# Hyena spectra laid out with two phases side by side, each piece moved by one transfer of 128 partitions, and more projection products ahead of the first spectrum

## The chip, the cores and the metric

The kernel runs on one core of one Trainium2 chip. Its time is the device time of one execution in microseconds (us); it is the median of several executions. A profile is one further execution, recorded by the hardware profiler. The core has a matrix engine (TensorE, PE in the profile; PEld is its weight load), three elementwise engines (VectorE, DVE; ScalarE, ACT; GpSimd, POOL), a queue engine (SyncE, SP), and 16 DMA engines that move data between main memory (HBM) and the on-chip memory. A DMA is issued from a queue (here SP's, or ACT's) and is carried out by DMA engines. On-chip tiles have up to 128 partitions (rows).

## What is computed

One layer of a hybrid encoder for 2048 positions of width 1024, all in float32. The part that the change touches is the Hyena group: 512 channels, a convolution over the whole length by FFT, gated, twice in a row (order 2), with filters that a small sine network makes.

```python
u = rms_norm(h); proj = u @ w_in                         # 1024 -> 3600 columns
hy = short_conv(proj[:, :1536])                          # v, gate 1, gate 2
spec = rfft(two-sided filter, length 4096)               # sine FFN times a decay window, 2 orders
z = hy[:, :512]
for o, gate in enumerate((hy[:, 512:1024], hy[:, 1024:1536])):
    conv = irfft(rfft(z, n=4096) * spec[o], n=4096)[:2048]
    z = gate * (conv + z * skip[o])
y_hy = group_rms_norm(z)
# beside it: an mLSTM group of 4 heads; then output projection, cross-attention, MLP, final norm
```

## The kernel before

Every large product is split into three TensorE products (`mm3`, L357, L360, L361: high by high, low by high, high by low part), 128 x 128 weights against 512 columns. The order in which the program is written is made by `weave` (end of the listing): two generators run in turn, each yields an amount of work, and the one that is behind by its own total goes on. The filters (`filters`) are woven into the first projection sweeps with the weights 140 and 102, and `hyena` into the rest of the projection and the mLSTM's preparation with 499 and 297. A `yield 24` in `hyena` (L1000) therefore lets the other generator go ahead by 24/297 x 499 = 40 of its units before the first spectrum; 1 unit was meant as about 1 us. A scheduler then orders the instructions of each engine.

**The FFT.** Length 4096 is split into 64 frequencies k (of 32 rows n) and 64 residues. Position = 64 n + 16 q + j: q is the phase (0 to 3), j the residue (0 to 15). The steps are:

1. `filters`, function `front`: for a pair of residues j2 (two values of j) and an order o, four banks of TensorE (one for each phase) give 128 rows: 64 rows of frequencies for each of the two residues. They are copied into two tiles `st[h]`, each with phases 2h and 2h + 1 side by side (128 partitions x 2 x 512), and `by_phase` (L339) stores them into the scratch tensor `fs`. Eight pairs, two orders, two tiles: 32 tiles of 512 KB.
2. `hyena`, function `spectrum` (L988): the same for the signal, from tiles that `load1` (L924) reads from `hy`, into the scratch `zs`. 16 tiles for each order; h = 0 is stored from ACT's queue, h = 1 from SP's.
3. The loop over 16 blocks of frequencies: `load_filter` and `load2` (L931, L939) read a block of `fs` and of `zs` (function `of_block`, L908), two products with a table (`c_dm`) finish the transform over the 64 residues, the filter is multiplied in, a product with `c_em` goes back, and `back` (L978) stores the block to the scratch `zg` from ACT's queue. A block needs all residues of its frequencies, so the first block waits for every store of step 2.
4. The loop over eight pairs of residues: `load3` (L963) reads two tiles of `zg` through `by_phase`, and a gate tile from `hy`; the product with `e2` finishes the inverse; the gate is multiplied in. For order 0 the result goes straight into `spectrum(1, ...)`, for order 1 it is normalised and stored to `yh` (L1064).

**The scratch layout before** is (64 frequencies, 4 phases, 16 residues, 512 channels). A tile of `by_phase` has the two residues in its two partition halves, so it is moved by two transfers of 64 partitions, with two rows of 2 KB to each partition. `of_block` is moved by two transfers of 64 partitions too, one for each frequency parity g; the tiles of `hy` and `yh` by four transfers of 32 partitions, one for each phase.

The tile pools matter: `filters` has 7 tiles of 512 KB (`ta`), of which the decay windows hold up to 4, and `hyena` has 10. A tile that is being stored cannot be used again before the store has landed.

A place that the change leaves alone, but that the prediction uses: `halves` in the preparation of the memory tokens (L679 to L685) loads eight pieces of 64 KB from the scratch `rows` into quarters of the tile `rp`. In the tile a piece has 32 partitions; in the scratch it is read as 4 groups with a step of their own, of 8 rows of 2 KB each: `by_half = rows.rearrange("i (d s n h) t -> s (i d) n (h t)", d=2, s=2, n=8)`, then `dma_start(out=rp[32 * q:32 * q + 32, s], in_=by_half[s])`.

Of the kernel before, what the change touches and what calls it, by code (L numbers as in the profile page):

```python
# [21 lines left out]
CH = 512  # L22
# [6 lines left out]
def shape_constants():  # L29
    f32 = np.float32  # L30
    ang = f32(TWO_PI / L) * np.arange(L, dtype=f32)
    tl = np.linspace(0.0, 1.0, L, dtype=f32)
    bands = np.linspace(1e-4, 15, 16, dtype=f32)
    arg = bands[:, None] * ang[None, :]
    feat = np.concatenate([tl[None], np.cos(arg), -np.sin(arg)], axis=0).astype(f32)
    back = (L - np.arange(L)) % L
    c_feat = np.concatenate([feat, feat[:, back]], axis=0)

    lo = math.log(1e-2) / 1.5
    hi = math.log(1e-2) / 0.3  # L40
    deltas = np.abs(np.linspace(lo, hi, CH, dtype=f32))
    win = np.exp(-(tl[:, None] * deltas[None, :]).astype(np.float64)).astype(f32)
    winb = win[back].copy()
    winb[0] = 0.0
    c_win = np.stack([win, winb], 0).reshape(2, 32, 4, 16, CH).transpose(0, 2, 1, 3, 4).reshape(2, L, CH)

    n1 = np.arange(32)
    kk = np.arange(16)
    f1 = np.zeros((2, 32, 4, 16, 2, 4))
    for par in range(2):  # L50
        th = 2 * np.pi * ((n1[:, None] * (2 * kk + par)[None, :]) % 64) / 64
        for h in range(4):
            f1[par, :, h, :, 0, h] = np.cos(th)
            f1[par, :, h, :, 1, h] = -np.sin(th)
            if par == 0:
                f1[0, :, h, 0, 1, h] = 1.0 - 2.0 * (n1 % 2)
    f1 = f1.reshape(2, 128, 128)
    wgt = np.full((2, 16, 2, 4), 2.0)
    wgt[0, 0] = 1.0
    e2 = f1.transpose(0, 2, 1) * (wgt.reshape(2, 128, 1) / 4096.0)  # L60
    own = f1.reshape(2, 32, 4, 16, 2, 4)[:, :, 0, :, :, 0].transpose(1, 0, 2, 3).reshape(32, 64)
    inv = e2.reshape(2, 16, 2, 4, 32, 4)[:, :, :, 0, :, 0].reshape(64, 32)

    n2 = np.arange(64)
    k2 = np.arange(64)

    def block(freq):
        th = 2 * np.pi * ((n2[:, None] * freq[None, :]) % 4096) / 4096
        return np.cos(th), np.sin(th)

    dm = np.zeros((32, 2, 64, 2, 64))
    for par in range(2):
        for k in range(16):
            k1 = 2 * k + par
            b = dm[par * 16 + k]
            if k1 > 0:
                c, s = block(k1 + 64 * k2)
                b[0, :, 0], b[1, :, 0], b[0, :, 1], b[1, :, 1] = c, s, -s, c
            else:
                c, s = block(64 * k2[:32])  # L80
                b[0, :, 0, :32], b[0, :, 1, :32] = c, -s
                b[0, :, 1, 0] = 1.0 - 2.0 * (n2 % 2)
                c, s = block(32 + 64 * k2[:32])
                b[1, :, 0, 32:], b[1, :, 1, 32:] = c, -s
    dm = dm.reshape(32, 128, 128)
    em = dm.transpose(0, 2, 1).copy()
    two = np.full((128, 1), 2.0)
    two[0] = two[64] = 1.0
    em[0] *= two
    c = {  # L90
        "c_feat": c_feat,
        "c_win": c_win,
        "c_f1": np.tile(own, (4, 1)),
        "c_e2": np.tile(inv, (2, 1)),
        "c_dm": dm.transpose(1, 0, 2),
        "c_em": em.transpose(1, 0, 2),
    }
    return {k: np.ascontiguousarray(v.astype(np.float32)) for k, v in c.items()}
# [30 lines left out]
class Prog:  # L129
# [101 lines left out]

    def filters(self):
        nc, tc, a = self.nc, self.tc, self.a
        sd = [self.dram(f"fs{o}", (64, 4, 16, CH)) for o in range(2)]
        sb, ta, tb = self.fsb, self.ta, self.tb
        if True:
            fw = sb.tile([128, 1280], F32, name="fw")
# [79 lines left out]
            for j2 in range(8):  # L317
                yield 9
                (wf, wb), nxt = nxt, windows(j2 + 1)
                for o in range(2):  # L320
                    st, es = [ta() for h in range(2)], []
                    for jj in range(2):
                        j = 2 * j2 + jj
                        pf, pb = self.hy(), self.hy()
                        self.beside((pf, hid[0:64, j], w3[0:64, o]), (pb, hid[64:128, j], w3[64:128, o]))
                        f, b = tb(), tb()
# [10 lines left out]
        self.fes.close()  # L337

    def by_phase(self, queue, d, j2, h, t, load=False):  # L339
        for jj in range(2):  # L340
            at, own = d[:, 2 * h:2 * h + 2, 2 * j2 + jj], t[64 * jj:64 * jj + 64]
            queue.dma_start(out=own if load else at, in_=at if load else own)

    def filters_open(self):
        self.fes = ExitStack()
# [554 lines left out]
    def hyena(self, es):  # L900
        nc, tc, a = self.nc, self.tc, self.a
        hy = self.dram("hy", (3, L, CH)).rearrange("s (n q j) c -> s q n j c", q=4, j=16)
        yh = self.dram("yh", (L, CH)).rearrange("(n q j) c -> q n j c", q=4, j=16)
        fs, sds, gds = ([self.dram(f"{n}{o}", (64, 4, 16, CH)) for o in range(2)] for n in ("fs", "zs", "zg"))
        own = [slice(64 * g, 64 * g + 64) for g in range(2)]
        phase = [slice(32 * q, 32 * q + 32) for q in range(4)]

        def of_block(d, g, k):  # L908
            return d[2 * k + g:2 * k + g + 3:2].rearrange("k q j c -> (q j) k c")

        sb = es.enter_context(tc.tile_pool(name="h_sb", bufs=1))

# [11 lines left out]
        def load1(j2):  # L924
            z = ta()
            js = slice(2 * j2, 2 * j2 + 2)
            for q in range(4):
                nc.sync.dma_start(out=z[phase[q]], in_=hy[0, q, :, js])
            return z

        def load_filter(o, i):  # L931
            dm = sb.tile([128, 2, 128], F32, tag="dm", name="dm", bufs=3)
            nc.sync.dma_start(out=dm, in_=a["c_dm"][:, 2 * i:2 * i + 2])
            t = ta()
            for g in range(2):
                nc.sync.dma_start(out=t[own[g]], in_=of_block(fs[o], g, 2 * i))
            return dm, t

        def load2(o, i):  # L939
            em = sb.tile([128, 2, 128], F32, tag="em", name="em", bufs=2)  # L940
            nc.sync.dma_start(out=em, in_=a["c_em"][:, 2 * i:2 * i + 2])
            t = ta()
            for g in range(2):
                nc.sync.dma_start(out=t[own[g]], in_=of_block(sds[o], g, 2 * i))
            return em, t

        def response(i, dm, t):
# [14 lines left out]
        def load3(o, j2):  # L962
            js = slice(2 * j2, 2 * j2 + 2)  # L963
            r = [ta() for h in range(2)]
            for h in range(2):
                self.by_phase(nc.sync, gds[o], j2, h, r[h], True)
            gate = ta()
            for q in range(4):
                nc.sync.dma_start(out=gate[phase[q]], in_=hy[1 + o, q, :, js])
            return r, gate  # L970

        held = []
# [7 lines left out]
        def back(m, i, em, y, gs, dst):  # L980
            pg = self.hy()
            nc.tensor.matmul(pg, em[:, m], y, start=True, stop=True)  # L982
            nc.scalar.copy(gs[:, m], pg)
            if m == 1:
                for g in range(2):
                    nc.scalar.dma_start(out=of_block(dst, g, 2 * i), in_=gs[own[g]])

        def spectrum(o, j2, z):  # L988
            st = [ta() for h in range(2)]
# [7 lines left out]
                self.by_phase(nc.sync if h else nc.scalar, sds[o], j2, h, st[h])  # L997

        q, fq = [load1(0), load1(1)], []
        yield 24  # L1000
        self.strict = True
        for j2 in range(8):
            yield 3.5
# [6 lines left out]
        for o in range(2):  # L1010
# [4 lines left out]
            for i in range(16):  # L1015
                yield 4.6
                dm, hr, hi = ready
                em, t = nxt
# [19 lines left out]
            for j2 in range(8):  # L1038
                yield 4.5 if o else 6.0
                js = slice(2 * j2, 2 * j2 + 2)  # L1040
                r, gate = nxt
                if j2 < 7:
                    nxt = load3(o, j2 + 1)
                pp = [self.hy() for jj in range(2)]
                self.beside(*((pp[jj][phase[q]], e2[own[jj]], r[q // 2][own[jj], q % 2])
                              for jj in range(2) for q in range(4)), pin=True)
                for jj in range(2):
                    nc.vector.tensor_tensor(gate[:, jj], pp[jj], gate[:, jj], ALU.mult)
                if o == 0:
                    late(lambda j2=j2, gate=gate: spectrum(1, j2, gate))  # L1050
                    if j2 > 5:
                        fq.append(load_filter(1, j2 - 6))
                    continue
                y = gate.rearrange("q j (g e) -> q (j g) e", g=8)
                sq = ta()
                sqv = sq.rearrange("q j (g e) -> q (j g) e", g=8)
                nc.gpsimd.tensor_tensor(sqv, y, y, ALU.mult)
                ms = sb.tile([128, 16], F32, tag="ms", name="ms", bufs=2)
                nc.vector.tensor_reduce(ms, sqv, AX.X, ALU.add)
                rv = self.bank_rsqrt(sb, ms, 64)  # L1060
                nc.vector.tensor_tensor(sqv, y, rv.unsqueeze(2).broadcast_to([128, 16, 64]), ALU.mult)
                for jj in range(2):
                    nc.gpsimd.tensor_tensor(sq[:, jj], sq[:, jj], ghy, ALU.mult)
                for q in range(4):  # L1064
                    nc.sync.dma_start(out=yh[q, :, js], in_=sq[phase[q]])
            late(None)

    def gates_open(self, es):
# [1026 lines left out]
def program(p):  # L2095
    with ExitStack() as ms:
        with ExitStack() as es:
# [15 lines left out]
            with ExitStack() as hs:  # L2113
# [2 lines left out]
                             among(chain(p.natural(0, (0, 1)), p.sweep((6, 7), 0, False),  # L2116
                                         p.natural(0, (2,), p.prep_mem, 2)), p.states(), 1),
                             p.turned_in(), take(n, 1), beside_each(n, take(m, 5)))
                weave(rest, p.hyena(hs), 499, 297, True)
            for _ in rest:  # L2120
                pass
        with ExitStack() as rs:
# [65 lines left out]
```

## Time and profile before

| | |
|---|---|
| median of 3 executions | 3109.29 us (3103.45 to 3109.89) |
| the profiled execution | 3107.95 us, of which its span is 3105.9 us |
| TensorE busy | 2983.7 us, 96% of the span |
| VectorE, ScalarE, GpSimd busy | 1945.9, 1496.0, 1124.2 us |
| moved by DMA | 607.08 MB, 195 GB/s over the span |
| mean granted TensorE clock | 0.983 |

The lines of the profile that are quoted below are of these kinds. A line of a table of windows has, for each engine, its busy time in that stretch and the number of instructions, then the TensorE clock that was granted, the mean busy share of the 16 DMA engines (it can pass 1 where packets overlap), and the GB/s that they moved. A line of one tile's instructions has the line of the kernel, the engine (SPq and ACTq are the DMA queues of SP and ACT, and the duration is that of the issue, not of the transfer), the number, the least, median and longest duration in ns, and the first and last start in us. A line of a DMA queue has its packets, its MB and the time that the packets took, as a share of 16 engines over the stretch asked for. A timeline's line has start, duration, engine, line, operation, and in brackets the idle time before it with what ended it.

### The profile page before, as it was taken

The page shows a single profiled execution, that of the slowest core. Times are in us where ns is not written, and L with a number is a line of the kernel's source. Part 1 is how long each engine was busy: PE and PEld are TensorE (multiplying, and loading weights), DVE is VectorE, ACT ScalarE, POOL GpSimd, SP SyncE. Part 2 cuts the span into 40 slices and gives each one's busy share as a digit, 9 for nine tenths or more (in the row PEclk, how much of TensorE's full clock was granted, in tenths as well). Part 3 has the DMA queues.
Part 4 walks back from the last instruction along what each step waited for, and adds up shares of the span by engine and source line. Part 5 has one row for each costly group of instructions (what it writes and reads, how often), then busy time and mean ns, then how long its engine had stood idle before and what let it go on. Part 6 is the DMA issues. An engine that isn't in the chain of part 4 may idle for free.

```text
span 3105.9 us, 44160 instructions
## 1 busy us (share of the span) xinstructions
PE 2983.7 (96%) x14799; PEld 2369.4 (76%) x14799; DVE 1945.9 (63%) x3442; ACT 1496.0 (48%) x2930; POOL 1124.2 (36%) x798
## 2 busy tenths in 40 slices
PE   9999699999999898999999999999999999999998
PEld 7666467776676666888887888888888888888876
DVE  8865365457556346877665666557555676566695
ACT  6443365534556235565544455556555543333335
POOL 0121011200222243333132337766456475244653
PEclk9999899999999899999999999999999999999999
DMA  6565778687777996565475657657644565354534
GB/s 222 187 179 172 217 228 240 184 234 224 230 208 239 277 318 217 154 199 173 132 265 192 211 165 241 204 180 232 203 155 152 178 211 178 109 166 116 160 102 163
DMA packets 458955, 607.08 MB, mean 195 GB/s; under 512 B 41310, under 2 KB 251102, under 8 KB 457704
## 3 DMA queue, kind: packets, MB, share of 16 engines
q1 hardware_dynamic: 418532, 546.47, 56.5%
q10 hardware_dynamic: 40196, 57.79, 5.6%
q8 instruction: 117, 1.92, 0.3%
q14 instruction: 110, 0.90, 0.1%
HBM read 401.70 MB, written 202.41 MB: 195 GB/s over the span
## 4 chain that ended last, share of the span: by engine, by line
PE 82%; DMA 8%; DVE 5%; issue 2%; ACT 2%; SPq 1%; POOL 1%; ACTq 0%; DVEq 0%; POOLq 0%
PE mm L357 17%; PE mm L361 17%; PE mm L360 17%; PE hy L361 6%; PE hy L357 6%; PE hy L360 6%; PE hy L173 2%; PE mm L951 2%; PE hy L1027 1%; PE hy L982 1%; DMA a<-zg 1%; DMA a<-hy 1%; PE mm L738 1%; PE mm L709 1%; PE hy L1319 1%
## 5 line engine op out<-in xcount | busy, mean ns | idle before, releaser
L1687 ACT CAST ah<-w 128x512 fp32r<-128x512 f32 x284 | 176.9, 624 | 300.4 <-PE hy L360 155.6
L1688 DVE TENSOR_TENSOR bl<-wr,bh 128x512 fp32r<-128x512 f32 x213 | 237.2, 1117 | 130.0 <-ACT bh L1687 125.6
L368 DVE TENSOR_TENSOR wl<-wn,wh 128x512 fp32r<-128x512 f32 (+1 forms) x296 | 214.4, 771 | 96.0 <-ACT wh L368 95.7
L357 PE MATMUL mm<-xh,wh 128*128 128x512 f32 x640 | 265.9, 417 | 4.8 <-ACT xh L368 2.8
L1032 POOL TENSOR_TENSOR b<-b,a 128x512 f32<-128x512 f32 x64 | 85.8, 1343 | 503.2 <-ACT b L1030 406.6
L360 PE MATMUL mm<-xl,wh 128*128 128x512 f32 x640 | 255.2, 399 | 5.0 <-DVE xl L368 5.0
L361 PE MATMUL mm<-xh,wl 128*128 128x512 f32 x640 | 254.6, 398 | 0.0
L1687 ACT CAST bh<-wr 128x512 fp32r<-128x512 f32 x232 | 143.9, 622 | 228.6 <-PE mm L361 171.7
L1688 DVE TENSOR_TENSOR al<-w,ah 128x512 fp32r<-128x512 f32 x236 | 214.2, 908 | 55.9 <-ACT ah L1687 55.9
L361 PE MATMUL mm<-bh,al 128*128 128x512 f32 x576 | 223.7, 391 | 4.1 <-DVE al L1688 4.1
L357 PE MATMUL mm<-bh,ah 128*128 128x512 f32 x576 | 225.9, 392 | 0.1
L360 PE MATMUL mm<-bl,ah 128*128 128x512 f32 x576 | 225.1, 391 | 0.0
L368 ACT CAST wh<-wn 128x512 fp32r<-128x512 f32 (+1 forms) x296 | 165.2, 621 | 111.6 <-PE mm L361 50.0
L360 PE MATMUL mm<-act,wh 128*128 128x512 f32 x512 | 201.6, 394 | 0.0
L357 PE MATMUL mm<-act,wh 128*128 128x512 f32 x512 | 199.6, 396 | 1.3 <-ACT wh L368 1.2
L361 PE MATMUL mm<-act,wl 128*128 128x512 f32 x512 | 200.0, 392 | 0.3 <-DVE wl L368 0.3
L357 PE MATMUL hy<-bh,ah 128*128 128x512 f32 x448 | 175.2, 391 | 0.0
L360 PE MATMUL hy<-bl,ah 128*128 128x512 f32 x448 | 174.6, 390 | 0.0
L361 PE MATMUL hy<-bh,al 128*128 128x512 f32 x448 | 174.4, 390 | 0.0
L357 PEld LDWEIGHTS mm<-xh,wh 128*128 128x128 f32 x640 | 121.3, 190 | 54.3 <-issue 17.8
L357 PE MATMUL mm<-wh,xh 128*128 128x256 f32 (+1 forms) x512 | 155.2, 303 | 3.5 <-DVE st L203 2.0
L360 PEld LDWEIGHTS mm<-xl,wh 128*128 128x128 f32 x640 | 121.5, 190 | 45.3 <-issue 14.1
(380 smaller groups left out, 8090.4 us busy)
## 6 DMA issues: line engine op xcount, KB each, us to landing
wr<-hc SPq DMA_DIRECT2D x224, 256.0 KB
w<-in_ff_w_dram SPq DMA_DIRECT2D x172, 256.0 KB
hc<-wn SPq DMA_DIRECT2D x128, 256.0 KB
wn<-in_w_in_dram SPq DMA_DIRECT2D x100, 256.0 KB
hc<-q SPq DMA_DIRECT2D x96, 256.0 KB
fs<-a SPq DMA_DIRECT2D x64, 256.0 KB
a<-fs SPq DMA_DIRECT2D x64, 256.0 KB
a<-zs SPq DMA_DIRECT2D x64, 256.0 KB
```

The lines of the kernel that those rows point to most:

```text
L173: b = self.nc.tensor.matmul(*products[-1], start=True, stop=True)
L357: first = mm(ps, lh, rh, start=start, stop=False)
L360: mm(ps, lh, rl, start=False, stop=False)
L361: self.last = mm(ps, ll, rh, start=False, stop=stop)
L368: both = (self.nc.scalar.copy(hi, src), self.nc.vector.tensor_tensor(lo, src, hi.bitcast(F32), ALU.subtract))
L709: mul(p[:, m], w[:, k, ms], mt[k // 4][:, k % 4], start=k == 0, stop=k == 7)
L738: mul(p, t[:, m, ms], o_[:, m, ds], start=m == 0, stop=m == 1)
L951: nc.tensor.matmul(pp, dm[:, m], t[:, m], start=True, stop=True)
L982: nc.tensor.matmul(pg, em[:, m], y, start=True, stop=True)
L1032: nc.gpsimd.tensor_tensor(xt, xt, hi[:, m], ALU.mult)
L1687: self.nc.scalar.copy(hi, src)
L1688: eng.tensor_tensor(lo, src, hi.bitcast(F32), ALU.subtract)
```

## The change

The scratch tensors `fs`, `zs` and `zg` become (64 frequencies, 16 residues, 4 phases, 512 channels): phases 2h and 2h + 1 of a residue now lie side by side as 4 KB. `by_phase` moves its tile by one transfer of 128 partitions; on the scratch side it walks the two residues, then the 64 frequencies, then 4 KB. `of_block` is one transfer of 128 partitions too; since the residue now comes before the phase there, the rows of the tables `c_dm` and `c_em` are put into the same order (n2). The tiles of `hy` and `yh` are moved by one transfer for all four phases instead of four. The amounts of data and the arithmetic stay. Besides, `yield 24` becomes `yield 52` and the weight of `hyena` 325 instead of 297, so the other generator goes ahead by 52/325 x 499 = 80 units before the first spectrum.

```diff
-    n2 = np.arange(64)
+    n2 = np.arange(64).reshape(4, 16).T.reshape(64)
...
-        sd = [self.dram(f"fs{o}", (64, 4, 16, CH)) for o in range(2)]
+        sd = [self.dram(f"fs{o}", (64, 16, 4, CH)) for o in range(2)]
...
     def by_phase(self, queue, d, j2, h, t, load=False):
-        for jj in range(2):
-            at, own = d[:, 2 * h:2 * h + 2, 2 * j2 + jj], t[64 * jj:64 * jj + 64]
-            queue.dma_start(out=own if load else at, in_=at if load else own)
+        at = d[:, 2 * j2:2 * j2 + 2, 2 * h:2 * h + 2].rearrange("k j q c -> j k q c")
+        queue.dma_start(out=t if load else at, in_=at if load else t)
...
-        def of_block(d, g, k):
-            return d[2 * k + g:2 * k + g + 3:2].rearrange("k q j c -> (q j) k c")
+        def of_block(d, i):
+            return d[4 * i:4 * i + 4].rearrange("(k g) j q c -> g (j q) k c", g=2)
...
-            for q in range(4):
-                nc.sync.dma_start(out=z[phase[q]], in_=hy[0, q, :, js])
+            nc.sync.dma_start(out=z, in_=hy[0, :, :, js])
...
-            for g in range(2):
-                nc.sync.dma_start(out=t[own[g]], in_=of_block(fs[o], g, 2 * i))
+            nc.sync.dma_start(out=t, in_=of_block(fs[o], i))
...
-            for q in range(4):
-                nc.sync.dma_start(out=gate[phase[q]], in_=hy[1 + o, q, :, js])
+            nc.sync.dma_start(out=gate, in_=hy[1 + o, :, :, js])
...
-                for g in range(2):
-                    nc.scalar.dma_start(out=of_block(dst, g, 2 * i), in_=gs[own[g]])
+                nc.scalar.dma_start(out=of_block(dst, i), in_=gs)
...
-        yield 24
+        yield 52
...
-                for q in range(4):
-                    nc.sync.dma_start(out=yh[q, :, js], in_=sq[phase[q]])
+                nc.sync.dma_start(out=yh[:, :, js], in_=sq)
...
-                weave(rest, p.hyena(hs), 499, 297, True)
+                weave(rest, p.hyena(hs), 499, 325, True)
```

**SP, the filters' stores** (`a` is a tile of the pool, `fs_388` and `fs_389` the scratch of the two orders, `wn` weights of the projection, `hy` the scratch of the projected columns). Before:

```order
L342 DMA fs_389<-a 64x2x512 x4
L829 DMA hy<-st 126x4x128 x2
L526 DMA xt<-in_x_t_dram 128x2x512 x4
L294 DMA a<-in_c_win_dram 128x1024
L342 DMA fs_388<-a 64x2x512 x4
L294 DMA a<-in_c_win_dram 128x1024
L397 DMA wn<-in_w_in_dram 128x2x256 x4
```

Now:

```order
L341 DMA fs_389<-a 2x64x1024 x2
L828 DMA hy<-st 126x4x128 x2
L525 DMA xt<-in_x_t_dram 128x2x512 x4
L294 DMA a<-in_c_win_dram 128x1024
L341 DMA fs_388<-a 2x64x1024 x2
L294 DMA a<-in_c_win_dram 128x1024
L396 DMA wn<-in_w_in_dram 128x2x256 x4
```

The places in the queue are the same; four stores with 64 rows outermost became two with 2 outermost. The same happens to `zs` and, as loads, to `zg`.

**PE, ahead of the first spectrum** (`b` against `f_394` is a front of the filters, `fw` against `hid` makes the filters, `a` against `f_2776` or `f_2744` is the first spectrum, `mm` is a projection product). Before:

```order
L173 MATMUL hy<-fw,hid 128x512
L186 MATMUL hy<-fw,hid 128x512
L173 MATMUL hy<-b,f_394 32x512
L186 MATMUL hy<-b,f_394 32x512 x15
L173 MATMUL hy<-a,f_2776 64x512
L186 MATMUL hy<-a,f_2776 64x512 x7
L357 MATMUL mm<-xh,wh 128x512
L360 MATMUL mm<-xl,wh 128x512
```

Now the first spectrum has projection products right ahead of it:

```order
L356 MATMUL mm<-xh,wh 128x512
L359 MATMUL mm<-xl,wh 128x512
L360 MATMUL mm<-xh,wl 128x512
L173 MATMUL hy<-a,f_2744 64x512
L186 MATMUL hy<-a,f_2744 64x512 x7
L356 MATMUL mm<-xh,wh 128x512
```

Before, the last front is followed by the first spectrum with no projection product between; 36, 0 and 0 stand between the last four fronts. Now 47, 52 and 61 stand between them and 60 between the last front and the first spectrum: 184 products more are ahead of it. Between two spectra there are 24 in both.

More of the change, by code (lines that the diff above doesn't have):

```diff
@@ L903, in hyena @@
         yh = self.dram("yh", (L, CH)).rearrange("(n q j) c -> q n j c", q=4, j=16)
-        fs, sds, gds = ([self.dram(f"{n}{o}", (64, 4, 16, CH)) for o in range(2)] for n in ("fs", "zs", "zg"))
+        fs, sds, gds = ([self.dram(f"{n}{o}", (64, 16, 4, CH)) for o in range(2)] for n in ("fs", "zs", "zg"))
         own = [slice(64 * g, 64 * g + 64) for g in range(2)]
         phase = [slice(32 * q, 32 * q + 32) for q in range(4)]
-        def of_block(d, g, k):
-            return d[2 * k + g:2 * k + g + 3:2].rearrange("k q j c -> (q j) k c")
+        def of_block(d, i):
+            return d[4 * i:4 * i + 4].rearrange("(k g) j q c -> g (j q) k c", g=2)
         sb = es.enter_context(tc.tile_pool(name="h_sb", bufs=1))
@@ L942, in load2 @@
             t = ta()
-            for g in range(2):
-                nc.sync.dma_start(out=t[own[g]], in_=of_block(sds[o], g, 2 * i))
+            nc.sync.dma_start(out=t, in_=of_block(sds[o], i))
             return em, t
@@ L984, in back @@
             if m == 1:
-                for g in range(2):
-                    nc.scalar.dma_start(out=of_block(dst, g, 2 * i), in_=gs[own[g]])
+                nc.scalar.dma_start(out=of_block(dst, i), in_=gs)
         def spectrum(o, j2, z):
```

## The prediction

> **What bounds the kernel now.** I read the busy times and the chain first, then the stages, then the DMA engines.
>
> ```profile
> PE 2983.7 (96%) x14799; PEld 2369.4 (76%) x14799; DVE 1945.9 (63%) x3442; ACT 1496.0 (48%) x2930; POOL 1124.2 (36%) x798
> PE 82%; DMA 8%; DVE 5%; issue 2%; ACT 2%; SPq 1%; POOL 1%; ACTq 0%; DVEq 0%; POOLq 0%
> ```
>
> TensorE bounds the kernel as a whole; only 8% of the chain is DMA. The change adds no arithmetic, so it matters only where a DMA ends the wait. The tiles say when the moved transfers run.
>
> ```profile
> L342 SPq DMA_DIRECT2D fs<-a x64: 574/599/1732, 121.8 to 338.4; - x64
> L928 SPq DMA_DIRECT2D a<-hy x32: 302/422/2217, 343.1 to 384.4; - x32
> L342 SPq DMA_DIRECT2D zs<-a x32: 575/620/2284, 354.3 to 769.9; - x32
> L944 SPq DMA_DIRECT2D a<-zs x64: 573/605/1447, 409.2 to 980.4; - x64
> L342 SPq DMA_DIRECT2D a<-zg x64: 573/592/1962, 641.3 to 1131.2; - x64
> L1065 SPq DMA_DIRECT2D yh<-a x32: 302/417/717, 1059.8 to 1185.9; - x32
> ```
>
> From these I cut four stages: A, the filters' stores (122 to 340); B, the first spectra (340 to 410, when the first blocks are read); D, the middle, where `zg` of order 0 is read and `zs` of order 1 stored (637 to 775); F, the last inverse (1015 to 1190). Between them lie the block loops, whose `of_block` transfers stay 128 or 64 rows deep.
>
> ```profile
> core 0: us, PE busy (x) PEld busy (x) DVE busy (x) ACT busy (x) POOL busy (x), PEclk, DMA share, GB/s
> 122.00:340.00 218.00, 195.61 (x1250) 127.73 (x1248) 130.70 (x199) 86.51 (x149) 44.00 (x30) 0.95 0.61 182
> 340.00:410.00 70.00, 60.98 (x351) 42.91 (x352) 28.50 (x46) 29.07 (x46) 0.00 (x0) 0.91 0.88 275
> 637.00:775.00 138.00, 129.50 (x853) 96.60 (x852) 85.24 (x226) 54.85 (x92) 0.00 (x0) 1.00 0.86 245
> 1015.00:1190.00 175.00, 152.83 (x782) 114.50 (x781) 79.74 (x249) 51.02 (x147) 62.28 (x50) 0.93 0.95 289
> ```
>
> The share of the DMA engines is 0.61 to 0.95 in them: little is spare if the same bytes leave through fewer engines.
>
> **How many engines a transfer gets.** Before, a `by_phase` transfer begins with 64 rows on both sides. Now it begins with 128 partitions on the tile's side and with 2 residues on the scratch's; the tiles of `hy` and `yh` begin with 128 and 4. The trace has one transfer of this form, the eight loads into `rp`: 32 partitions on one side, 4 groups on the other.
>
> ```profile
> L685 SPq DMA_DIRECT2D rp<-rows x8: 598/610/1248, 985.5 to 993.7; - x8
> 985.55 5.16 SPq L685 DMA_DIRECT2D rp<-rows  x5
> DMA packets 27, 0.05 MB, mean 100 GB/s; under 512 B 2, under 2 KB 3, under 8 KB 27
> q1 hardware_dynamic: 27, 0.05, 27.0%
> ```
>
> The last two rows are the window 991.5 to 992, in which nothing but these loads was left to move, five of them already issued. With a backlog of several transfers the 16 engines are busy 27%, that is four of them, and move 100 GB/s, 25 GB/s each. Had each load taken another four engines, or all, the backlog would have gone at several times that. So a transfer of 4 outer groups is confined to four engines, consecutive ones to the same four. For contrast, four stores of `fs` in the window 327.2 to 332.6:
>
> ```profile
> DMA packets 560, 1.04 MB, mean 192 GB/s; under 512 B 61, under 2 KB 61, under 8 KB 559
> q1 hardware_dynamic: 559, 1.02, 66.0%
> ```
>
> Those used 66% of the 16 on average, start included. I conclude that the new `by_phase` transfer runs on two engines and the new `hy` and `yh` transfers on four, always the same ones. Two outer groups is not in the trace; I extend the row of four to it.
>
> A page of the Trainium skill has the rule behind this: "DMA: Bandwidth & Descriptors", section "Why a DMA increments its semaphore by 16 and not by 1", says that a transfer is spread over the largest number of engines, at most 16, that divides the slowest dimension of both sides, and that queues of this kind take the lowest-numbered ones. By it the sum is the one below; the trace agrees for 4 of 16 engines.
>
> The same page, section "Rules for kernel authors", speaks for the change: it advises one transfer of 128 partitions in place of two on partition halves, since both halves use the same engines anyway. By that rule alone the time would be the second rival's.
>
> **The price of a transfer.** 512 KB (524,288 bytes) over two engines at 25 GB/s is 10.5 us; over four, 5.2 us. Bounds for the rate:
>
> ```profile
> DMA packets 658, 1.66 MB, mean 416 GB/s; under 512 B 102, under 2 KB 258, under 8 KB 657
> q1 hardware_dynamic: 418532, 546.47, 56.5%
> ```
>
> The fastest stretch (1124 to 1128) gives 416/16 = 26 GB/s an engine. The mean of the whole span gives 546.47 MB in 56.5% of 16 x 3105.9 us, 19.5 GB/s. I take 25, since two engines alone do not contend with fourteen others, as the four of `rp` did not.
>
> What the two engines must carry besides is a sixteenth of all other traffic in the stage:
>
> ```profile
> DMA packets 32283, 39.70 MB, mean 182 GB/s; under 512 B 2192, under 2 KB 20688, under 8 KB 32267
> DMA packets 12633, 19.22 MB, mean 275 GB/s; under 512 B 1720, under 2 KB 6424, under 8 KB 12627
> DMA packets 27547, 33.81 MB, mean 245 GB/s; under 512 B 5596, under 2 KB 16911, under 8 KB 27535
> DMA packets 37490, 50.58 MB, mean 289 GB/s; under 512 B 3136, under 2 KB 26432, under 8 KB 37478
> ```
>
> (A, B, D, F in this order.) The sum by stage, as work of the two most loaded engines:
>
> - A: 32 stores of `fs` x 10.5 = 336; other traffic 39.70 - 16.78 = 22.9 MB, a sixteenth at 25 GB/s is 57. Together 393 us in a stage of 218: 175 too many.
> - B: 16 stores of `zs` x 10.5 = 168; 8 loads of `hy` x 5.2 = 42; others 6.6 MB, 17. Together 227 in 70: 157 too many.
> - D: 16 loads of `zg` 168, 16 stores of `zs` 168, 8 gates 42, others 12.8 MB 32. Together 410 in 138: 272 too many.
> - F: 16 loads of `zg` 168, 8 gates 42, 8 stores of `yh` 42, others 33.8 MB 85. Together 336 in 175: 161 too many.
>
> 765 us in all. Why they are not hidden: a store holds its tile until it lands, and with 7 tiles in the filters and 10 in `hyena` only two or three can be under way, 21 to 32 us of work; the first block needs every store of `zs`; and each loaded pair of residues is waited for by the next product. Everything behind these transfers on SP's queue (projection weights, `c_win`, `dm`, `em`) has a share on the same two engines and lands later too.
>
> **The moved products.** Ahead of the first spectrum the trace has TensorE idle for 14.04 us:
>
> ```profile
> 333.81 1.06 PE L173 MATMUL hy<-b,f 32*32 32x512 f32 x1
> 349.02 1.08 PE L173 MATMUL hy<-a,f 32*64 32x512 f32 x1 [14.04 <-DMA a<-hy]
> 352.36 0.39 PE L357 MATMUL mm<-xh,wh 128*128 128x512 f32 x1
> 353.06 0.39 PE L357 MATMUL mm<-xh,wh 128*128 128x512 f32 x1
> ```
>
> 184 products more now stand there. Three of them take 353.06 - 352.36 = 0.70 us, so it is 43 us of work, which comes out of the block loop and the rest of the stages and runs while the filters' stores drain. I take off 43 us. Less than nothing is not to be had from it; at least it covers the 14 us.
>
> **What else is saved.** Half the issues of these transfers go, on SP and on ACT.
>
> ```profile
> L986 ACTq DMA_DIRECT2D zg<-a x64: 582/616/707, 437.3 to 1014.5; - x64
> ```
>
> On ACT that is 32 x 0.616 = 20 us of issue; ACT is 48% busy and its queue has 0% of the chain, so I count nothing. At most it would give the 20 us.
>
> **The sum.** The profiled execution took 3107.95 us, 1.3 below the median of 3109.29. 3108 + 765 - 43 = **3830 us**, 23% slower. Both ends: only the moved transfers at 26 GB/s, with all other traffic fitted in elsewhere, are 323 + 201 + 363 + 242 = 1129 us, less the stages' 601 and 43: 3593. At 19.5 GB/s the 1366 us become 1751: 3108 + 1751 - 601 - 43 = 4215.
>
> **Rivals.**
>
> *DMA and TensorE take turns.* If a weight load behind two or three stores stops TensorE, no new store is made, the two engines run dry, and the stage takes the sum of both. TensorE's busy time in the four stages is 196 + 61 + 130 + 153 = 539 us, so fully in turns 4370. It decides as soon as the backlog (21 to 32 us) is longer than the lead of a weight load. For it: weights share SP's queue. Against it: they are fetched a whole group ahead, and the stage's slower pace lengthens that lead.
>
> *The transfers spread over 16 engines after all.* Then the halves are only joined: the 14.04 us ahead of the first spectrum go, and of the chain's 1% for `zg` loads (31 us) perhaps half: 3108 - 14 - 15 = 3080, faster. Its point: whether the outermost dimension of 2 is what counts. For it: the bytes and the partitions are those of a well-spread transfer. Against it: the row of `rp`.
>
> ```profile
> PE mm L357 17%; PE mm L361 17%; PE mm L360 17%; PE hy L361 6%; PE hy L357 6%; PE hy L360 6%; PE hy L173 2%; PE mm L951 2%; PE hy L1027 1%; PE hy L982 1%; DMA a<-zg 1%; DMA a<-hy 1%; PE mm L738 1%; PE mm L709 1%; PE hy L1319 1%
> ```
>
> *Narrow, but stores are hidden.* If stores drain beside the block loops, only loads count: D 168 + 42 + 32 = 242 against 138, F 168 + 42 + 85 = 295 against 175, A and B nothing. 3108 + 104 + 120 - 14 = 3318. Against it: the blocks wait for the stores of `zs`, and the tiles are too few.
>
> **Chances.** Forecast (3600 to 4130) 0.80; in turns beyond that 0.08; stores hidden 0.06; spread, faster 0.04; no change 0.02. The range is the forecast's, from the lower bound up to where half of TensorE's time in turns would lead (3830 + 270 = 4100) and somewhat over; the rivals stay outside. A measurement of this kernel tells about 0.2% from no change. Slower by more than that 0.94, within 0.02, faster 0.04.
>
> **What would show it.** Every transfer posts one 4-byte packet for each engine that it uses. The page now counts
>
> ```profile
> DMA packets 458955, 607.08 MB, mean 195 GB/s; under 512 B 41310, under 2 KB 251102, under 8 KB 457704
> ```
>
> 512 transfers on 16 engines become 96 on 2, 96 on 16 and 32 on 4: 8192 such packets become 1856, so the count under 512 B falls to about 34,970; spread over 16 it would be about 36,700. The DMA share in the four stages should fall to about 0.2 to 0.4 while TensorE waits for `fs`, `zs` and `zg`; the stages should last about 390, 230, 410 and 340 us; the block loops and all after the last inverse should keep their lengths. Wrong is the forecast if the count stays near 36,700, or if the stages lengthen but TensorE is then found waiting for projection weights rather than for these tiles.

## The result, and the profile after

The changed kernel takes 3877.34 us (3875.79 to 3878.73, 4 runs), the kernel before 3106.91 us beside it: a ratio of 1.248, 95% interval 1.2458 to 1.2502. The forecast was 3830 us. The page of the changed kernel gives its busy times, the chain by engine and the count of DMA packets:

```profile
PE 3076.8 (79%) x14799; PEld 2411.7 (62%) x14799; DVE 1936.6 (50%) x3442; ACT 1489.7 (38%) x2928; POOL 1130.9 (29%) x798
PE 52%; DMA 8%; SPq 4%; DVE 2%; issue 1%; ACT 1%; POOL 1%; ACTq 0%; DVEq 0%; POOLq 0%
DMA packets 440328, 607.03 MB, mean 157 GB/s; under 512 B 34974, under 2 KB 244766, under 8 KB 439080
```

TensorE is busy 79% instead of 96%. The same bytes move. The packets under 512 B, which hold one completion packet for each engine of each transfer, are 34,974; the forecast said about 34,970 for pieces on two and tiles on four engines, and 36,700 for 16.

The same stages as in the prediction, in the table of windows of the changed kernel (A, B, the first block loop, D, the second block loop, F). Each is cut near the same events as before, to within 5 us: the first load of `hy`, the first load of `zs` in each order, the first load of `zg` in each order, and the end of the last stores.

```profile
122.00:532.00 410.00, 265.57 (x1437) 174.46 (x1435) 143.50 (x218) 101.03 (x171) 46.98 (x30) 0.81 0.31 104
532.00:762.00 230.00, 71.84 (x339) 46.25 (x339) 34.40 (x55) 32.73 (x52) 0.00 (x0) 0.64 0.26 91
762.00:989.00 227.00, 221.05 (x1244) 169.99 (x1245) 132.25 (x208) 133.86 (x241) 43.89 (x32) 0.98 0.64 205
989.00:1378.00 389.00, 143.57 (x688) 92.34 (x686) 79.92 (x213) 53.18 (x87) 2.09 (x2) 0.66 0.23 81
1378.00:1600.00 222.00, 215.18 (x1100) 159.32 (x1101) 132.40 (x237) 124.28 (x216) 57.55 (x50) 0.97 0.72 229
1600.00:1960.00 360.00, 167.46 (x758) 119.02 (x756) 81.52 (x256) 52.18 (x164) 64.69 (x49) 0.72 0.43 139
```

A, B, D and F last 410, 230, 389 and 360 us instead of 218, 70, 138 and 175: 788 us more. Between them the first block loop keeps its 227 us, and the second is 18 us shorter (222 instead of 240). Together these 770 us are the 769 us by which the span grew (3875.2 against 3105.9). In the long stages the DMA share is 0.23 to 0.43, lower than before, and TensorE waits. These are among the longest of its waits, named by what ended them, over the whole execution, with one of ScalarE (us in all, times, longest):

```profile
PEld hy L173 <- issue: 272.8, 55, 34.2
PE hy L173 <- DMA a<-zg: 162.3, 9, 33.3
PE mm L725 <- ACT o L715: 90.5, 5, 33.5
ACT a L313 <- DMA fs<-a: 101.9, 8, 23.8
PE hy L173 <- DMA a<-hy: 58.4, 3, 24.1
PE hy L1021 <- DMA a<-zs: 55.2, 2, 33.6
PE mm L947 <- DMA a<-fs: 45.0, 2, 26.0
```

L173 is the product that begins a front of the filters, a spectrum or an inverse. Narrow means: on two engines. `a<-zg` are narrow loads, `a<-hy` tiles on four engines, and `fs<-a` narrow stores whose tiles ScalarE needs again. `a<-zs` and `a<-fs` are block loads, which are not narrow but come behind the narrow transfers. The row with "issue" names nothing that the profile saw, and it is not to be added to those of PE: in D, PE's own rows alone come to 227 of its 245 us of idle time.

L725 is a product of the cross-attention's preparation, which runs beside the last inverse, in F; the change does not touch its transfers. There TensorE waits 90.5 us for the copies `o` that this product needs, and only 35.5 us for `a<-zg`. For most of the time that ScalarE stands idle before these copies, the profile names the end of a DMA, of several kinds (`a<-hy` 36.2 us, `va<-vd` 34.4, a weight `wm` 28.0). So in A, B and D the longest wait is for moved tiles (58.8 us for those that ScalarE fills after `fs<-a`, 58.4 for `a<-hy`, 126.8 for `a<-zg`), and in F it is for work beside them.

A window of stage B in which only two pieces are moving, one from each queue:

```profile
DMA packets 128, 0.52 MB, mean 52 GB/s; under 512 B 0, under 2 KB 0, under 8 KB 128
q1 hardware_dynamic: 64, 0.26, 6.4%
q10 hardware_dynamic: 64, 0.26, 6.4%
```

This is 700 to 710 us. SP's queue (q1) and ACT's (q10) both have a piece of `zs` in flight, and together they keep 12.8% of 16 engines busy: two engines, at 26 GB/s each, shared half and half. At their 52.4 GB/s a piece of 512 KB that moves alone would take 10.0 us.

### The profile page after: what moved, and what is told of

Its sections match the earlier page's. It is cut to its first block, busy times and chain, and to the rows that moved or that the text cites. A ratio compares the mean times of both kernels' runs of the same rounds, so it can differ in the third digit from the quotient of the medians.

```text
span 3875.2 us, 43797 instructions
## 1 busy us (share of the span) xinstructions
PE 3076.8 (79%) x14799; PEld 2411.7 (62%) x14799; DVE 1936.6 (50%) x3442; ACT 1489.7 (38%) x2928; POOL 1130.9 (29%) x798
## 2 busy tenths in 40 slices
DMA packets 440328, 607.03 MB, mean 157 GB/s; under 512 B 34974, under 2 KB 244766, under 8 KB 439080
## 4 chain that ended last, share of the span: by engine, by line
PE 52%; DMA 8%; SPq 4%; DVE 2%; issue 1%; ACT 1%; POOL 1%; ACTq 0%; DVEq 0%; POOLq 0%
PE mm L356 10%; PE mm L360 10%; PE mm L359 10%; PE hy L360 5%; PE hy L356 5%; PE hy L359 5%; SPq L964 1%; DMA wm<-in_xa_wv_dram 1%; DMA kn<-st 1%; DMA zs<-a 1%; DMA va<-vd 1%; DMA wm<-in_xa_wq_t_dram 1%; DMA a<-zg 1%; SPq L416 1%; PE mm L708 1%
## 5 line engine op out<-in xcount | busy, mean ns | idle before, releaser
L356 PE MATMUL mm<-xh,wh 128*128 128x512 f32 x640 | 281.5, 441 | 78.3 <-ACT st L201 25.8
L359 PE MATMUL mm<-xl,wh 128*128 128x512 f32 x640 | 269.9, 422 | 2.1 <-DVE xl L367 2.1
L360 PE MATMUL mm<-xh,wl 128*128 128x512 f32 x640 | 266.5, 417 | 0.0
L356 PEld LDWEIGHTS mm<-xh,wh 128*128 128x128 f32 x640 | 130.9, 205 | 144.7 <-issue 31.0
L333 POOL TENSOR_TENSOR b<-b 128x512 f32<-128x512 f32 x32 | 52.2, 1630 | 437.9 <-DVE b L332 434.2
L173 PE MATMUL hy<-a,e 64*32 64x512 f32 x32 | 25.6, 895 | 176.1 <-DMA a<-zg 162.3
```

Source lines behind the costliest of these rows:

```text
L173: b = self.nc.tensor.matmul(*products[-1], start=True, stop=True)
L333: nc.gpsimd.tensor_tensor(b, f, b, ALU.subtract)
L356: first = mm(ps, lh, rh, start=start, stop=False)
L359: mm(ps, lh, rl, start=False, stop=False)
L360: self.last = mm(ps, ll, rh, start=False, stop=stop)
```

## The experiments

In these, "cost" is the time above the kernel with split pieces (`split_all`, the first experiment), each taken against the kernel before as run beside it.

**Split the pieces, keep the rest of the change.** Theory: the outermost dimension sets the number of engines and nothing else is slow. Rivals: the layout with 4 KB rows is slow, or the moved products are.

```diff
-        at = d[:, 2 * j2:2 * j2 + 2, 2 * h:2 * h + 2].rearrange("k j q c -> j k q c")
-        queue.dma_start(out=t if load else at, in_=at if load else t)
+        for jj in range(2):
+            at, own = d[:, 2 * j2 + jj, 2 * h:2 * h + 2], t[64 * jj:64 * jj + 64]
+            queue.dma_start(out=own if load else at, in_=at if load else own)
...
-            nc.sync.dma_start(out=z, in_=hy[0, :, :, js])
+            for q in range(4):
+                nc.sync.dma_start(out=z[phase[q]], in_=hy[0, q, :, js])
```

(And so for the gates and `yh`.)

> Theory (few engines): the number of DMA engines follows from the outermost dimension of both sides, and nothing else of the change is slow. Here the new scratch layout, its rows of 4 KB, the joined block transfers and the moved products stay; only the pieces go back to two transfers of 64 rows, and the tiles of hy and yh to four of 32. Expected 3080 us (3060 to 3100), packets under 512 B 39,770 (96 fewer transfers than before, 16 each). Rival (layout): rows of 4 KB in the new layout are slow in main memory whatever the engines; then it stays near 3800 us. Rival (order): the moved products cost the time; then it also stays near 3800 us.

Measured 3081.77 us (3079.08 to 3087.83), ratio to before 0.993 (0.9914 to 0.9945). Its packets:

```profile
DMA packets 445130, 607.06 MB, mean 197 GB/s; under 512 B 39774, under 2 KB 249566, under 8 KB 443880
```

The layout, the 4 KB rows, the joined block transfers and the moved products are all still there, and the kernel is faster than before. Both rivals fall; the loss is the joined pieces and tiles alone.

**One transfer a piece, but contiguous in the scratch.** The scratch is laid out as (8 pairs, 2 halves, 2 residues, 64 frequencies, 2 phases, 512), so that the piece has 128 outermost on both sides.

```diff
-        at = d[:, 2 * j2:2 * j2 + 2, 2 * h:2 * h + 2].rearrange("k j q c -> j k q c")
+        at = d[j2, h].rearrange("j k q c -> (j k) q c")
...
-            return d[4 * i:4 * i + 4].rearrange("(k g) j q c -> g (j q) k c", g=2)
+            return d[:, :, :, 4 * i + 2 * m:4 * i + 2 * m + 2].rearrange("a h j g q c -> (a h j) (g q) c")
```

(The block transfers are two again, the tiles of `hy` and `yh` four, and the rows of the tables follow the layout.)

> Another scratch layout, in which a whole piece (two residues by 64 frequencies by 4 KB) is contiguous, so one transfer of 128 partitions moves it, with 128 outermost on both sides; the block transfers are two of 128 partitions (32 outermost on the scratch side), hy and yh four of 32. Theory (few engines): 16 engines again, 3080 us (3060 to 3110), packets under 512 B 39,770. Rival (one transfer of 512 KB for a whole piece is slow as such, because its tile is free later): 3200 us or more.

Measured 3087.17 us (3084.43 to 3094.08), ratio 0.9948 (0.993 to 0.9965), and the count under 512 B is the expected one (39,774). So one transfer of 128 partitions for a whole piece is not slow as such. What counts is that the scratch side began with 2.

The Trainium skill, "DMA: Bandwidth & Descriptors", section "Rules for kernel authors", advises one transfer of 128 partitions in place of two on halves. The runs disagree for the change's layout (3877 us). For this one they show no harm and no gain: 3087 us against the 3082 us of the split kernel, whose layout is another; two transfers on halves were not run in this layout.

**The moved products alone, in three kernels.**

```diff
-        yield 24
+        yield 52
...
-                weave(rest, p.hyena(hs), 499, 297, True)
+                weave(rest, p.hyena(hs), 499, 325, True)
```

In the kernel before:

> The kernel before with the moved products alone (yield 52, weight 325). Theory (few engines): the 14 us that TensorE was idle ahead of the first spectrum go, 3093 us (3080 to 3107). Rival (order): the moved products cost hundreds of us; 3400 us or more.

Taken back from the changed kernel:

> The changed kernel without the moved products (yield 24, weight 297 again). The prediction's term: 184 products cover 43 us of stores, so without them 3920 us. Rival (as in the kernel before, where the idle time came back in later stages): no gain, 3877 us within 10.

Taken back from the split kernel:

> The kernel with split pieces, without the moved products: the layout and the joined block transfers alone. If the moved products are worth nothing here either: 3082 us (3076 to 3088). Rival: with the shorter last inverse their 14 us of covered idle time now reach the end, so without them 3092 to 3100 us.

Measured: in the kernel before 3105.29 against 3105.2 us, ratio 1.000 (0.999 to 1.0011), nothing. In the changed kernel 3876.91 us without them and 3877.34 with, nothing. In the split kernel 3093.95 us without them (ratio 0.9969, 0.9959 to 0.9979) and 3081.77 with: 12 us. My 14 us for the kernel before and 43 us for the changed one were both wrong. The windows of the kernel before with the moved products (`before_more`) show where the idle time went (A, B, D, F; compare the four rows in the prediction):

```profile
122.00:340.00 218.00, 210.93 (x1313) 142.60 (x1312) 136.11 (x210) 90.58 (x155) 42.82 (x29) 0.99 0.62 187
340.00:420.00 80.00, 75.47 (x431) 53.11 (x429) 35.59 (x56) 37.66 (x58) 1.28 (x1) 0.96 0.82 255
655.00:785.00 130.00, 113.57 (x665) 77.29 (x664) 68.78 (x197) 45.31 (x75) 2.09 (x2) 0.93 0.86 243
1024.00:1191.00 167.00, 140.94 (x710) 101.53 (x708) 74.79 (x233) 43.53 (x129) 58.46 (x43) 0.94 0.96 293
```

TensorE's idle time in A and B fell from 22 + 9 to 7 + 5 us, but in D and F it rose from 9 + 22 to 16 + 26: the products that filled the gap ahead of the first spectrum are missing there, where the DMA engines are 0.86 and 0.96 busy. Over the whole span TensorE is idle 11 us less (111 instead of 122), but the same 14,799 matmuls keep it busy 10 us longer (2993.8 instead of 2983.7 us); in D its granted clock is 0.93 instead of 1.00. The last stores of `yh` say the same, first `before_more`, then the split kernel without and with the moved products (1185.9 us in the kernel before):

```profile
L1065 SPq DMA_DIRECT2D yh<-a x32: 302/419/1196, 1068.9 to 1187.6; - x32
L1062 SPq DMA_DIRECT2D yh<-a x32: 302/398/825, 1056.1 to 1177.1; - x32
L1062 SPq DMA_DIRECT2D yh<-a x32: 302/424/1219, 1051.2 to 1160.1; - x32
```

The layout with joined block transfers ends the inverse 9 us earlier by itself, and with it the moved products are worth another 17. These are single executions, and the one without the moved products was 6 us above its median, so some of the 17 may belong to the 9. Which of the two, rows of 4 KB or joined blocks, gives the 9 us was not tried.

**Each kind of piece narrow by itself.** Base: the split kernel; one kind is joined again, here `fs`.

```diff
     def by_phase(self, queue, d, j2, h, t, load=False):
+        if d is self.s["fs0"] or d is self.s["fs1"]:
+            at = d[:, 2 * j2:2 * j2 + 2, 2 * h:2 * h + 2].rearrange("k j q c -> j k q c")
+            queue.dma_start(out=t if load else at, in_=at if load else t)
+            return
         for jj in range(2):
```

> Base: the kernel with split pieces (3081.8 us). Only the 32 filter pieces are joined again to one transfer with 2 outermost. Price of a piece from the changed kernel's trace: 52.4 GB/s over two engines, 10.0 us. Theory (throughput: a stage lasts as long as the work of its two busiest engines, narrow pieces and a sixteenth of the rest): 320 + 55 = 375 us in stage A, which lasts 229 in the base: +146, 3228 us. Rival (queueing: a piece's time comes on top, since all behind it waits): 320 less the 40 that they took on 16 engines, +280, 3362 us.

> Base as before; only the 32 stores of zs are joined (half of them from ACT's queue). Throughput: B 160 + 26 = 186 us against 75, D 160 + 61 = 221 against 130: +202, 3284 us. Queueing: +280, 3362 us. Stores hidden: 3082 us.

> Base as before; only the 32 loads of zg are joined. Throughput: D 160 + 61 = 221 us against 130, F 160 + 101 = 261 against 159: +193, 3275 us. Queueing: +280, 3362 us. If only loads mattered, this one would hold nearly all of the 795 us.

By throughput, a stage lasts as long as the work of its two busiest engines; by queueing, the time by which each piece is longer comes on top. Each kernel was executed twice.

| narrow | time, us | before beside it | cost | by throughput | by queueing |
|---|---|---|---|---|---|
| 32 stores of `fs` | 3255.38 | 3102.78 | 176 | 146 | 280 |
| 32 stores of `zs` | 3330.25 | 3102.78 | 251 | 202 | 280 |
| 32 loads of `zg` | 3333.04 | 3102.78 | 254 | 193 | 280 |

The stores of `zs` cost as much as the loads of `zg`, and those of `fs` cost 176 us, so the rival "narrow, but stores are hidden" falls. Each lies between the two sums. Together with the tiles on four engines (103, below) they make 784 us; all at once the changed kernel has 794 (770 above before, and the split kernel 23 below it). The costs nearly add.

**The tiles of `hy` and `yh` on four engines**, in the kernel before and in the split kernel.

```diff
-            for q in range(4):
-                nc.sync.dma_start(out=z[phase[q]], in_=hy[0, q, :, js])
+            nc.sync.dma_start(out=z, in_=hy[0, :, :, js])
```

> The kernel before with only the tiles of hy and yh moved by one transfer (4 outermost). Theory (few engines): four engines carry 42 us for 8 tiles. With a sixteenth of all other traffic at 25 GB/s that is 80 us in stage B (70 long), 116 in D (138), 189 in F (175): 3107 + 10 + 14 = 3131 us (3112 to 3175), packets under 512 B 39,390. Rival (rows): these rows were 4 KB before, so nothing changes, 3107 us within 0.3%, or 5 to 10 us less through fewer issues.

> The kernel with split pieces, but the tiles of hy and yh still in one transfer (4 outermost, four engines). Queueing, from the measured 3222 - 3105 = 117 us of the same in the kernel before: 3082 + 117 = 3199 us. Throughput by the work of the four engines: 3082 + 24 = 3106 us.

Measured 3222.27 us (ratio 1.038, 1.0361 to 1.0399) and 3184.41 us (1.0259, 1.0245 to 1.0273): a cost of 117 and 103 us, where the sum by busiest engines said 24. Rows in the scratch were 4 KB before and after, so the rows are not it. In the first of the two the last store of `yh` is issued at 1290.9 us instead of 1185.9, and the share of the DMA engines in the last inverse is far from full (0.95 before):

```profile
1015.00:1190.00 175.00, 119.07 (x602) 92.41 (x601) 59.91 (x146) 46.41 (x90) 39.48 (x33) 0.84 0.76 214
1190.00:1304.00 114.00, 91.16 (x422) 62.45 (x420) 46.83 (x149) 30.97 (x97) 36.18 (x27) 0.91 0.63 200
```

So a transfer on few engines costs more than those engines' lack of time. TensorE's longest waits in this run are 31.4 and 25.3 us for the copies `o` of the cross-attention's preparation and 19.3 us for a table (`em`), none of them a tile on four engines. This fits that what stands behind a narrow transfer is late by its length; no run shows it transfer by transfer.

**Eight engines.** Every eight frequencies of the scratch are padded by one, so that a half piece begins with 8.

```diff
-        sd = [self.dram(f"fs{o}", (64, 16, 4, CH)) for o in range(2)]
+        sd = [self.dram(f"fs{o}", (8, 9, 16, 4, CH)) for o in range(2)]
...
-            at, own = d[:, 2 * j2 + jj, 2 * h:2 * h + 2], t[64 * jj:64 * jj + 64]
+            at, own = d[:, 0:8, 2 * j2 + jj, 2 * h:2 * h + 2], t[64 * jj:64 * jj + 64]
```

(And so for `zs` and `zg`; the block transfers skip the padding.)

> The kernel with split pieces (3081.8 us), in which the scratch has every eight frequencies padded by one, so each of the 192 half pieces has 8 outermost on the scratch side. Theory (few engines): eight engines; packets under 512 B 39,774 - 192 x 8 = 38,238. What it costs tells the two sums apart. Throughput (a stage is as long as the work of its busiest engines): A 16.8/8/26 + 55 = 136 us against 229, B 66 against 75, D 122 against 130, F 141 against 159: nothing, 3082 us (to 3095). Queueing (each piece's time beyond that on 16 engines is added): 96 pieces x (2.5 - 1.25) = 120 us, with the 0.8 to 0.9 of that measured for two and four engines about 100: 3180 us.

Measured 3165.88 us (ratio 1.0185, 1.0162 to 1.0209), a cost of 84 us; the packets are the expected ones:

```profile
DMA packets 443594, 607.06 MB, mean 192 GB/s; under 512 B 38238, under 2 KB 248030, under 8 KB 442344
```

Throughput said nothing, queueing 100 to 120. The padding alone, with the pieces on 16 engines, was not run. Beside the time by which a transfer would be longer than on 16 engines (worked out at 26 GB/s an engine), the cost is

| engines | longer by | in all | cost | share |
|---|---|---|---|---|
| 2 (96 pieces) | 8.75 us | 840 us | 681 us | 0.81 |
| 4 (32 tiles) | 3.75 us | 120 us | 103 and 117 us | 0.86 and 0.98 |
| 8 (96 pieces) | 1.25 us | 120 us | 84 us | 0.70 |

So 0.7 to 1.0 of the added length reaches the end, for each number of engines. Of the three kinds on two engines, `fs` alone has 0.63 (176 of 280 us), `zs` and `zg` 0.90 and 0.91. All these transfers come from SP's and ACT's queues.

**The same narrow pieces from another queue.** GpSimd's queue issues the 32 joined stores of `fs`.

```diff
-            queue.dma_start(out=t if load else at, in_=at if load else t)
+            self.nc.gpsimd.dma_start(out=at, in_=t)
```

> As narrow_fs, but the 32 joined filter pieces are issued from GpSimd's queue instead of SP's. Theory (the same two engines each time are the cost): if that queue gives successive pieces other engines, two or three pieces move side by side, the stage is near the base's and the time 3082 to 3120 us; the DMA rate while pieces alone move rises over 52 GB/s. Rival (one piece's 10 us is the cost, whichever engines): about narrow_fs's time. If this queue too uses the same two engines, also about narrow_fs's time, at 52 GB/s.

Measured 3140.79 us (ratio 1.0121, 1.0092 to 1.015), a cost of 61 us instead of 176. In 319 to 323 us only one such pair of stores moves beside a little else:

```profile
DMA packets 206, 0.42 MB, mean 105 GB/s; under 512 B 18, under 2 KB 126, under 8 KB 206
q0 software_dynamic: 80, 0.33, 20.0%
q1 hardware_dynamic: 126, 0.09, 8.4%
```

q0 is GpSimd's queue: 20.0% of 16 engines is 3.2, so two pieces move on different engines at the same time, 0.33 MB in 4 us, 82 GB/s, where SP's and ACT's queues gave 52 together. So two thirds of the cost of the narrow `fs` is that SP's pieces take the same two engines each time, together with what waits on SP's queue behind them. The rest, 61 us, was not split between the 10 us of a piece and GpSimd's own work. The number of packets under 512 B does not give the engines here: it is 67,934, and 38,814 with the same pieces on SP's queue.

The Trainium skill, "DMA: Bandwidth & Descriptors", section "Why a DMA increments its semaphore by 16 and not by 1", says that SP's and ACT's queues take the lowest-numbered engines and GpSimd's goes round. The two windows agree as far as they go: SP and ACT share two engines, and two pieces from GpSimd have more than two. No view here shows which engines they are.

## Why the prediction was right, and where it was not

- **Two and four engines: right.** Extended from the row of `rp` (4 outer groups, four engines), it held for 2 and for 8, by the counts of packets. The time also came from it: with wide outermost dimensions the same data take 3082 and 3087 us.
- **25 GB/s an engine: right.** Measured 26.2 (52.4 GB/s on two).
- **The stages: the total right, by balance.** 765 us were expected. A came out 192 us over instead of 175, B 160 instead of 157, D 251 instead of 272, F 185 instead of 161, together 788; the second block loop, which was to keep its length, gave 18 back. The four stages are close to what two engines carry at the measured 26.2 GB/s, narrow transfers and a sixteenth of the rest (25.9, 8.4, 10.4 and 33.2 MB): 382 us of 410 in A, 220 of 230 in B, 385 of 389 in D, 319 of 360 in F.
- **"Too many", that is, only the work above a stage's length counts: near enough for all pieces at once, wrong as a rule.** With four and eight engines the busiest ones had time to spare, and the kernel still lost 84 to 117 us. For each kind of narrow piece alone the sum by the busiest engines came out 17 to 24% short (146, 202 and 193 of 176, 251 and 254 us). For all at once it was 765 of 794, where the full added length, 840 + 120 us, would have been too much. The cost goes with the length of each transfer, most of which reaches the end as long as the transfers share the same engines.
- **The moved products, -43 us: wrong, 0 us.** This term is 43 of the 47 us by which the forecast was too low. I took the products as cover for the stores. The run without them (`after_24`) has its first load of `zs` at 743.2 us instead of 761.8, so they were not even fully covered there; it has its last store of `yh` at 1943.8 instead of 1950.1 and ends no earlier. What they cost ahead is given back later. That they were taken out of waits for the same two engines fits this but was not tested apart. The 14 us of the second rival were 0 in the kernel before and 12 in the split kernel.
- **The layout, with fewer issues and joined blocks, counted as nothing: off by 11 us.** The split kernel without the moved products is 11 us faster than before. The second rival's 3080 us was met by the split kernel (3082): 12 for the moved products, where I had 14, and 11 for the layout and the joins, where I had 15 for half of the waits for `zg`. The second of these is luck: which part of the layout gives the 11 was not tried.
- **The rivals.** Stores hidden: shown wrong by the narrow `zs`. In turns: A lasts 410 us, 17 over the forecast's 393 and 28 over the 382 at the measured rate, far from the 589 of taking turns. Whether these are turns stays open. TensorE's rows name no weight of the projection. The sign that would have spoken against the forecast did come in part, in F: there TensorE waits longer for the cross-attention's preparation (L725, and 21.2 us for its weight `wm`) than for the moved tiles.

## What to carry to other kernels

Before joining DMAs, look at the outermost dimension of both sides as the transfer walks them: where it is 2, two engines do the work, the same two for SP's and ACT's queues, and here 96 such transfers and 32 on four engines cost a quarter of the kernel's time. Choose the scratch layout so that the outermost dimension is wide on both sides, as the 32, 64 and 128 of the kernels at 3082 and 3087 us. And work that is moved to fill one wait is worth something only if the place it leaves does not wait too.

## What had not been expected

The issue itself becomes long. In the kernel before, the issues of `zs` and `zg` on SP's queue had a median of 0.6 us; these are the ones of the changed kernel (least, median and longest in ns):

```profile
L341 SPq DMA_DIRECT2D zs<-a x16: 491/7733/14063, 557.2 to 1345.2; - x16
L341 SPq DMA_DIRECT2D a<-zg x32: 493/4536/10835, 989.1 to 1864.8; - x32
L341 ACTq DMA_DIRECT2D zs<-a x16: 490/500/606, 556.9 to 1331.5; - x16
```

SP stands for up to 14 us in one such issue, and everything behind it is not even issued. The chain now gives SPq 4% instead of 1%, for issues of several kinds. The other half of `zs`, issued from ACT, stays at 0.5 us, so it is not the two engines alone; how much must stand in a queue for its issues to become long was not worked out. I had only counted the wait in the DMA queue.

The granted TensorE clock falls in the stages that wait, to 0.64 in B and 0.66 in D (0.91 and 1.00 before), and the busy time of the same 14,799 matmuls grows from 2983.7 to 3076.8 us. What lies behind these stages hardly changes: from the last store of `yh` to the end it is 1920 us before (3105.9 - 1185.9) and 1925 after (3875.2 - 1950.1). Whether the lower clock lengthens the stages themselves, in which TensorE waits anyway, was not tested.
